# Retention scores times centred values: one fp32 product against three fp32r products of split parts, with the prompt's last 16 tokens stacked on 48 rows

## The chip, the cores and the metric

One NeuronCore of a Trainium2 chip runs one launch of the kernel. The metric is the device time of that launch in microseconds. The engines are TensorE (PE, with its weight loads shown apart as PEld), VectorE (DVE), ScalarE (ACT), GpSimd (POOL) and SyncE (SP, which issues most DMAs). Each works through its own queue in order, and the engines wait for each other through semaphores.

## The reference, cut to what matters

One step of a two-layer decoder: a pooling mixer, an MLP, a retention mixer with 8 heads, another MLP. 272 prompt tokens (16 of them learned) and 8 sample tokens run together. The change lies in the retention of the prompt:

```python
def retention_chunk(q, k, v, s, log_gamma):
    ...
    scores = jnp.einsum('bihd,bjhd->bhij', q, k) * decay[None]
    inner = jnp.einsum('bhij,bjhv->bihv', scores, v)
    ...
    s_new = s * s_dec[None, :, None, None] + jnp.einsum(
        'bjhd,bjhv->bhdv', k * k_dec[None, :, :, None], v).astype(s.dtype)
    return inner + cross, s_new

def retention_layer(x, pos, s, norm_g, w_in, w_out, log_gamma, n_lead):
    ...
    y = head_norm(o).reshape(b, t, RET_VDIM) * jax.nn.silu(g)   # head_norm: (o - mean) / std per head
    return x + y @ w_out, s
```

Since `head_norm` takes a mean over the 512 values of a head away from each token's output, the kernel takes that mean from each row of v first: "centred values". Scores times centred values is then the centred output of the prompt. The kernel computes the prompt in one piece (causal, 272 tokens) and not in chunks.

## The kernel before, in words

**Units.** The weights come as 388 units of 128x2048 numbers (1 MB, `raw`), loaded by SP in a fixed order (`ORDER`). Each unit is split in two halves: ACT casts a half to fp32r (`wh`, L130), DVE takes the rest (`wl`, L131), and TensorE multiplies in three products, `wh` by the activations' high part, `wl` by the high part, `wh` by the low part (`mm_acc`, L152): 48 products of 264 or 280 columns a unit. `begin_unit` splits two units ahead; `wh` and `wl` have four buffers each, so the half of a unit can be split once the same half of the unit two before has been used.

**Retention.** A head is four v units, two k, two q (the second of each makes the rotary embedding, `rope_unit`: two DVE products into `rpb`, then two POOL operations), four gate units g, and with heads 2, 4 and 7 (`PAIRED`) eight output units "oo", which multiply the outputs (`YH`, `YL`) of two earlier heads. Head 2 takes heads 0 and 1, head 4 takes 2 and 3, head 7 takes 5 and 6; head 7's own output is used in four "o" units after it. `v_tokens` turns v token by token (transposes, L466) in three groups `j` of 128, 128 and 16 tokens, and makes `vh`, `vl` (split v) and `vc` (centred, fp32). The last 16 tokens are copied six times side by side first (`tail_copies`), so that they stand on 96 rows. `attention(h)` is a generator that runs a step after each of the next twelve or so units: keys turned and split (L516), scores (L525) times decay (`pr`, L528), eight sample tokens (`sample`, L533 to L547: `kv` on ACT, state update and reductions on DVE), `prompt_o` (L555: per head two halves of two 128-value blocks `i`, each with three products for `j`), `prompt_state` (L565, L566), then the output's norm: the mean over samples (`om`, L587), the squares `osq` (ACT) summed by POOL (L597) between the gate products (L599), `token_rstd` (L196 to L206), `spread` (L210), and `oc`, `yh`, `yl` (L617 to L619).

**Order.** The program is written in the order of units, but a list scheduler of the tile framework moves instructions by its own estimate of when each is ready. So the order on each engine is fixed when the program is built, and a buffer that two tiles share orders their users. `tmp` with tag `sq` has two buffers, used in `prep` and for `osq`; `so`, `kv`, `rows` and `rpb` have buffers of their own (`kv` two).

Of the kernel before, what the change touches and what calls it, by code (L numbers as in the profile page):

```python
# [10 lines left out]
F32 = mybir.dt.float32  # L11
F32R = mybir.dt.float32r
# [4 lines left out]
P = 128  # L17
# [18 lines left out]
RT = (128, 128, 96)  # L36
# [47 lines left out]
def trunk_step(ctx: ExitStack, tc: tile.TileContext, wst, xT_d, xtok_d, spool_d, xc_d, xs_d, gains_d, gB_d, band_d, cs_d,  # L84
# [270 lines left out]
    with tc.tile_pool(name="rp", bufs=1) as rp, tc.tile_pool(name="rs", bufs=3) as rsp, \  # L355
# [45 lines left out]
        def rope_unit(h, kind, i, cols):  # L401
            parts = begin_unit(kind)
            w = cols.stop - cols.start
            ps = mm_tile(w)
            mm_acc(ps, parts, 0, XH, XL, cols)
            if i == 1:
                b = rp.tile([P, 2, C], F32, tag="rpb", name="rpb")
            else:
                cur[kind] = rp.tile([P, 2, C], F32, tag=kind + "T", name=f"{kind}T{h}")
            t = cur[kind] if i == 0 else b  # L410
            nc.vector.tensor_tensor(out=t[:, 0, :w], in0=ps, in1=(sin if i else cos)[:, cols], op=ALU.mult)
            nc.vector.tensor_tensor(out=t[:, 1, :w], in0=ps, in1=(cos if i else sin)[:, cols], op=ALU.mult)
# [37 lines left out]
        def v_tokens(h, j):  # L450
            vT = cur["v"]
            if j == 0:
# [4 lines left out]
                               for t, n, dt in (("vh", 3, F32R), ("vl", 2, F32R), ("vc", 3, F32))]  # L457
                cur["acc"] = rp.tile([P, 6], F32, tag="acc", name="acc")
                cur["vcols"] = token_cols(vT, 4)
            vh, vl, vc = cur["vtok"]  # L460
            acc = cur["acc"]
            nt, nr = JT[j][1], RT[j]
            rt = rtok[:nr, j:j + 1]
            ps = att_ps()
            for i in range(4):
                nc.tensor.transpose(ps[:nr, i * P:(i + 1) * P], cur["vcols"](i, j), ident)  # L466
# [5 lines left out]
        def split(hi, lo, ps, nr, scale, r0):  # L472

            rows = slice(0, nr)
            nc.scalar.activation(out=hi[rows], in_=ps[rows], func=AF.Copy, scale=scale)
            if nr < P:
                rows, lo = slice(r0, r0 + 32), hi
            nc.vector.scalar_tensor_tensor(out=lo[rows], in0=ps[rows], scalar=scale[rows],
                                           in1=hi[rows].bitcast(F32), op0=ALU.mult, op1=ALU.subtract)

        def attention(h, last):
            qT, kT, vs, (vh, vl, vc) = cur["q"], cur["k"], cur["vs"], cur["vtok"]
# [9 lines left out]
            rows = rp.tile([4 * NS, P], F32, tag="rows", name="rows")  # L492
# [18 lines left out]
            for j in range(3):  # L511
# [5 lines left out]
                split(kdh[:, j], kdl[:, min(j, 1)], ps[:, off:off + DK], RT[j], kvec[:RT[j], h, j:j + 1], 32)  # L517
# [3 lines left out]
            pr = rp.tile([P, DC], F32, tag="pr", name="pr")  # L521
            off = 0
            for j, (t0, nt, q0, nq) in enumerate(JT):
                for i in range(2):
                    nc.tensor.matmul(ps[:nt, off:off + nq], kT[:, i, t0:t0 + nt], qT[:, i, q0:q0 + nq], start=(i == 0),  # L525
                                     stop=(i == 1))
                off += nq
            nc.vector.tensor_tensor(out=pr[:, 0:400], in0=ps[:, 0:400], in1=dec[:, 0:400], op=ALU.mult)  # L528
            nc.vector.tensor_tensor(out=pr[:16, 400:416], in0=ps[:16, 400:416], in1=dec[:16, 400:416], op=ALU.mult)
# [19 lines left out]
            def prompt_o(half):  # L549
                ps = att_ps()  # L550
                for q in range(2):
                    i = half * 2 + q
                    off = 0
                    for j, (_, nt, q0, nq) in enumerate(JT):
                        nc.tensor.matmul(ps[:, q * 256 + q0:q * 256 + q0 + nq], vc[:nt, j, i * P:(i + 1) * P],  # L555
                                         pr[:nt, off:off + nq], start=(j == 0), stop=(j == 2))
                        off += nq
                nc.scalar.copy(out=OC[:, half * 2:half * 2 + 2, 0:256], in_=ps.rearrange("p (a b) -> p a b", a=2))

            def prompt_state(i):  # L560
# [5 lines left out]
                nc.tensor.matmul(ps, kdh[:96, 2, ds_], vh[:96, 2], start=False, stop=True)  # L566
                so = rp.tile([P, DV], F32, tag="so", name="so")
# [109 lines left out]
def constants():  # L677
# [22 lines left out]
    for h in range(H):  # L700
        off = 0
        for j, (t0, nt, q0, nq) in enumerate(JT):
            i = np.arange(q0, q0 + nq) + NMETA
            d = i[None, :] - (t0 + np.arange(nt))[:, None]
            dec[h, :nt, off:off + nq] = np.where(d >= 0, np.exp(np.maximum(d, 0) * LG[h]), 0.0) / 16.0
            kd = np.exp((NTOK - 1 - t0 - np.arange(nt)) * LG[h]) / 16.0
            kvec[:RT[j], h, j] = kd if j < 2 else np.tile(kd / 2.0, 6)
# [73 lines left out]
```

## Time and profile before

| | us |
|---|---|
| three timed runs, median (lowest to highest) | 2490.84 (2489.76 to 2491.4) |
| the profiled execution: its own time | 2488.74 |
| the span of its trace (first to last instruction) | 2487.0 |
| PE busy in the span | 2469.3 |
| DVE, ACT, POOL busy | 1513.0, 1152.6, 365.8 |
| the chain that ended last: "PE mm L152", the largest of the few that it follows | 30% of the span |

A start of a row in the timeline is the start of the first instruction of the group; the difference between two starts is the pace, while the duration of a matmul holds the pipeline's depth too. A plain fp32 matmul stands in the trace as two records, an fp32r matmul as one.

### The profile page before, as it was taken

To read this page: it belongs to the slowest core of one execution; us is meant where nothing else is said; L and a number is where in the kernel's file an instruction comes from. 1 tells how busy PE (TensorE), PEld (TensorE's weight loads), DVE (VectorE), ACT (ScalarE), POOL (GpSimd) and SP (SyncE) were. 2 spreads that over 40 slices of the span, in tenths; PEclk is the share of its full clock that TensorE was granted. 3 is DMA by queue.
4 is the path that set the end of the run, shared out by engine and by line. 5 is a ranking of instruction groups with operands and counts; after the bars stand their busy time and mean duration, and the time that the engine had idled before them with its cause. 6 is when DMAs were issued, how large, how long until landed. Compare 5 with 4: busy or idle time off the path is not lost. (4 is left out here: it accounts for less than half of the span.)

```text
span 2487.0 us, 46663 instructions
## 1 busy us (share of the span) xinstructions
PE 2469.3 (99%) x19560; PEld 2448.0 (98%) x19560; DVE 1513.0 (61%) x2400; ACT 1152.6 (46%) x1668; POOL 365.8 (15%) x280
## 2 busy tenths in 40 slices
PE   9999999999999999999999999999999999999998
PEld 9999999999999999999999999999999999999998
DVE  7554554554455567786778586788654654554553
ACT  5433333333334456664665565656433333333443
POOL 4210110120022101011010101102200200200222
PEclk9999999999999999999999999999999999999999
DMA  6444544444444557866668495885554455545453
GB/s 240 171 174 170 184 168 172 170 170 170 170 171 171 181 212 270 324 251 247 237 251 331 170 326 191 304 308 185 177 187 179 179 186 185 178 181 186 180 180 118
DMA packets 90182, 509.97 MB, mean 205 GB/s; under 512 B 10288, under 2 KB 11568, under 8 KB 39848
## 3 DMA queue, kind: packets, MB, share of 16 engines
q1 hardware_dynamic: 89507, 505.92, 56.3%
q8 instruction: 153, 2.51, 0.4%
q10 hardware_dynamic: 432, 0.95, 0.1%
q14 instruction: 58, 0.48, 0.1%
q0 software_dynamic: 32, 0.12, 0.0%
HBM read 466.72 MB, written 41.15 MB: 204 GB/s over the span
## 5 line engine op out<-in xcount | busy, mean ns | idle before, releaser
L130 ACT CAST wh<-raw 128x1024 fp32r<-128x1024 f32 x776 | 799.8, 1050 | 1181.9 <-PE mm L152 660.0
L131 DVE TENSOR_TENSOR wl<-raw,wh 128x1024 fp32r<-128x1024 f32 x776 | 1000.5, 1321 | 101.8 <-ACT wh L130 100.8
L152 PE MATMUL mm<-xh,wh 128*128 128x280 f32 (+1 forms) x3584 | 491.6, 289 | 0.0
L152 PE MATMUL mm<-xl,wh 128*128 128x280 f32 (+1 forms) x3584 | 488.8, 288 | 0.1
L152 PE MATMUL mm<-xh,wl 128*128 128x280 f32 (+1 forms) x3584 | 487.1, 287 | 0.0
L152 PEld LDWEIGHTS mm<-xh,wh 128*128 128x128 f32 x3584 | 463.2, 188 | 1.8 <-ACT wh L130 0.2
L152 PEld LDWEIGHTS mm<-xl,wh 128*128 128x128 f32 x3584 | 463.3, 188 | 0.6 <-DVE xl L174 0.3
L152 PEld LDWEIGHTS mm<-xh,wl 128*128 128x128 f32 x3584 | 462.7, 188 | 0.3
L322 POOL TENSOR_TENSOR hf<-r 128x280 f32<-128x280 f32 (+1 forms) x128 | 185.3, 1448 | 1154.6 <-DVE r L318 1154.6
L348 DVE TENSOR_TENSOR xT<-mm,xT 128x280 f32<-128x280 f32 (+1 forms) x128 | 56.4, 441 | 401.4 <-PE mm L152 401.4
L152 PE MATMUL mm<-hh,wh 128*128 128x280 f32 (+1 forms) x2048 | 276.3, 287 | 0.0
L152 PE MATMUL mm<-hh,wl 128*128 128x280 f32 (+1 forms) x2048 | 276.2, 287 | 0.0
L152 PE MATMUL mm<-hl,wh 128*128 128x280 f32 (+1 forms) x2048 | 276.2, 287 | 0.0
L152 PEld LDWEIGHTS mm<-hh,wh 128*128 128x128 f32 x2048 | 263.8, 188 | 0.0
L152 PEld LDWEIGHTS mm<-hh,wl 128*128 128x128 f32 x2048 | 263.8, 188 | 0.0
L152 PEld LDWEIGHTS mm<-hl,wh 128*128 128x128 f32 x2048 | 263.7, 188 | 0.0
L318 DVE SCALAR_TENSOR_TENSOR r<-mm,rstd 128x280 f32<-128x280 f32 (+1 forms) x128 | 56.2, 440 | 303.5 <-PE mm L152 303.4
L540 ACT ACTIVATE kv<-bc,vs 128x256 f32<-128x256 f32 x256 | 110.0, 499 | 39.8 <-DMA bc<-rd 36.6
L545 DVE CUSTOM_DVE_ANT_0 bc<-s,bc 128x256 f32<-128x256 f32 x256 | 103.2, 417 | 2.0
L542 DVE SCALAR_TENSOR_TENSOR s<-s,kv 128x512 f32<-128x512 f32 x128 | 86.2, 684 | 21.6 <-ACT kv L540 20.2
L170 POOL TENSOR_TENSOR ssq<-ssq,sq 128x280 f32<-128x280 f32 (+1 forms) x56 | 71.1, 1269 | 180.9 <-ACT sq L168 160.7
L599 POOL TENSOR_TENSOR oc<-oc,gs 128x264 f32<-128x264 f32 x32 | 31.8, 1007 | 322.2 <-ACT ssq L593 322.2
(179 smaller groups left out, 1504.2 us busy)
## 6 DMA issues: line engine op xcount, KB each, us to landing
raw<-in_wst SPq DMA_DIRECT2D x388, 1024.0 KB, 4.9
s<-in_sret SPq DMA_DIRECT2D x64, 512.0 KB, 5.3
out_rs<-s SPq DMA_DIRECT2D x64, 512.0 KB, 7.0
bc<-rd SPq DMA_DIRECT2D x64, 256.0 KB, 8.8
out_rp<-so SPq DMA_DIRECT2D x16, 256.0 KB, 5.4
xT<-in_xT SPq DMA_DIRECT2D x4, 560.0 KB, 15.1
dec<-in_dec SPq DMA_DIRECT2D x8, 208.0 KB, 6.5
xa<-in_xtok SPq DMA_DIRECT2D x1, 1024.0 KB, 7.0
```

Of the source, the lines that this page charges most:

```text
L130: nc.scalar.copy(out=wh, in_=src)
L131: nc.vector.tensor_tensor(out=wl, in0=src, in1=wh.bitcast(F32), op=ALU.subtract)
L152: nc.tensor.matmul(ps, parts[s][z][:, kk, :], rhs[k][:, cols], start=(j == 0), stop=(j == len(todo) - 1))
L170: nc.gpsimd.tensor_tensor(out=ssq[:, cols], in0=ssq[:, cols], in1=sq[:, :w], op=ALU.add)
L318: nc.vector.scalar_tensor_tensor(out=r[:, :T], in0=ps, scalar=0.0, in1=rstd[:, cols], op0=ALU.max, op1=ALU.mult)
L322: nc.gpsimd.tensor_tensor(out=hf[:, :T], in0=r[:, :T], in1=r[:, :T], op=ALU.mult)
L348: nc.vector.tensor_tensor(out=xT[:, n, cols], in0=ps, in1=xT[:, n, cols], op=ALU.add)
L540: nc.scalar.activation(out=kv[:, i, :], in_=bc[:, 256:512], func=AF.Copy, scale=vs[:, 2 * z + i, b:b + 1])
L542: nc.vector.scalar_tensor_tensor(out=s[:, 2 * z:2 * z + 2], in0=s[:, 2 * z:2 * z + 2], scalar=GAMMA[h], in1=kv, op0=ALU.mult, op1=ALU.add)
L545: nc.vector.tensor_tensor_reduce(out=bc[:, 256:512], in0=s[:, i, :], in1=bc[:, 0:256], op0=ALU.mult, op1=ALU.add, scale=1.0, scalar=0.0, a ...
L599: nc.gpsimd.tensor_tensor(out=OC[:, i], in0=OC[:, i], in1=gates[h][:, i], op=ALU.mult)
```

## The change

- `vc` (fp32) is replaced by `vch`, `vcl` (its fp32r split), and `pr` by `prh`, `prl`; `pr` itself is now written over the decay table `dec`. `prompt_o` does three fp32r products for `j` = 0 and 1 and one for `j` = 2.
- For `j` = 2 the 16 tokens stand three times on 48 rows (before: six times on 96), and high and low parts are laid out on the three copies so that one product holds all three terms. This goes for the keys and values in `prompt_state` too; the transposes of the tail have 48 columns where they had 96, and the last score product has 48 columns where it had 16.
- `split` is rewritten, with one more DVE instruction for the keys' tail.
- Buffers are shared where they had been separate: `rows`, `so` and the scratch of `v_tokens` for `j` = 0 and 2 use one `so` buffer, the scratch for `j` = 1 takes a `kv` buffer, and the rotary `rpb` takes the two `sq` buffers of `tmp`.

```diff
-RT = (128, 128, 96)
+RT = (128, 128, 48)
...
             if i == 1:
-                b = rp.tile([P, 2, C], F32, tag="rpb", name="rpb")
+                b = [tmp.tile([P, C], F32, tag="sq", name="rpb")[:, :w] for _ in range(2)]
...
-            nc.scalar.activation(out=vc[:nt, j], in_=ps[:nt], func=AF.Copy, scale=rt[:nt], accum_out=acc[:nt, j:j + 1])
-            split(vh[:, j], vl[:, min(j, 1)], ps, nr, rt, 64)
-            nc.vector.tensor_scalar_mul(acc[:nt, 3 + j:4 + j], acc[:nt, j:j + 1], -1.0 / DV)
-            nc.scalar.activation(out=vc[:nt, j], in_=vc[:nt, j], func=AF.Identity, bias=acc[:nt, 3 + j:4 + j])
+            t = scratch(j)[:nr]
+            nc.scalar.activation(out=t, in_=ps, func=AF.Copy, scale=rt, accum_out=acc)
+            split(vh[:nr, j], vl[:nr, min(j, 1)], ps, rt, ALU.mult, False)
+            nc.vector.tensor_scalar_mul(neg, acc, -1.0 / DV)
+            split(vch[:nr, j], vcl[:nr, min(j, 1)], t, neg, ALU.add, False)
+
+        def scratch(j=0):
+            return rp.tile([P, DV], F32, tag="kv" if j == 1 else "so", name="so", bufs=2 if j == 1 else 1)
+
+        def split(hi, lo, x, s, op, left):
+            kw = {"func": AF.Copy, "scale": s} if op is ALU.mult else {"func": AF.Identity, "bias": s}
+            nc.scalar.activation(out=hi, in_=x, **kw)
+            rows = slice(0, P)
+            if hi.shape[0] < P:
+                rows, lo = slice(0, 32) if left else slice(32, 48), hi
+            nc.vector.scalar_tensor_tensor(out=lo[rows], in0=x[rows], scalar=s[rows], in1=hi[rows].bitcast(F32),
+                                           op0=op, op1=ALU.subtract)
+            if hi.shape[0] < P and left:
+                nc.vector.tensor_scalar_mul(hi[:16], x[:16], s[:16])
...
+            nc.vector.tensor_tensor(out=pr[:, hd], in0=ps[:, hd], in1=dec[:, hd], op=ALU.mult)
+            nc.scalar.copy(out=prh[:, hd], in_=pr[:, hd])
+            nc.vector.tensor_tensor(out=pr[:tr, tl], in0=ps[:tr, tl], in1=dec[:tr, tl], op=ALU.mult)
+            nc.vector.tensor_copy(prh[:tr, tl], pr[:tr, tl])
+            nc.vector.tensor_tensor(out=prh[:32, tl], in0=pr[:32, tl], in1=prh[:32, tl].bitcast(F32), op=ALU.subtract)
+            nc.vector.tensor_copy(prh[:16, tl], pr[:16, tl])
+            nc.vector.tensor_tensor(out=prl[:, hd], in0=pr[:, hd], in1=prh[:, hd].bitcast(F32), op=ALU.subtract)
...
-                    for j, (_, nt, q0, nq) in enumerate(JT):
-                        nc.tensor.matmul(ps[:, q * 256 + q0:q * 256 + q0 + nq], vc[:nt, j, i * P:(i + 1) * P],
-                                         pr[:nt, off:off + nq], start=(j == 0), stop=(j == 2))
+                    for j, (_, _, q0, nq) in enumerate(JT):
+                        for m, (a, b) in enumerate(((vch, prh), (vch, prl), (vcl, prh))[:3 if j < 2 else 1]):
+                            nc.tensor.matmul(ps[:, q * 256 + q0:q * 256 + q0 + nq], a[:RT[j], j, i * P:(i + 1) * P],
+                                             b[:RT[j], off:off + nq], start=(j + m == 0), stop=(j == 2))
...
-                nc.tensor.matmul(ps, kdh[:96, 2, ds_], vh[:96, 2], start=False, stop=True)
-                so = rp.tile([P, DV], F32, tag="so", name="so")
+                nc.tensor.matmul(ps, kdh[:RT[2], 2, ds_], vh[:RT[2], 2], start=False, stop=True)
+                so = scratch()
```

The shared buffers move instructions. Line numbers of the changed kernel are some 1 to 15 higher (L210 stays, L411 now stands for both rotary products, L491 becomes L497, L525 L533, L555 L570, L566 L581, L587 L602, L588 L603, L597 L612, L617 L632).

On PE in head 2, from the last products of its first gate unit (`xl`) to the first product with head 1's output (before `yh_11520`, after `yh_11593`; `yh_10480` and `yh_10521` are head 0's); before:

```order
L210 MATMUL sp<-dg,ones 128x264
...
L152 MATMUL mm<-xl_108,wh_1_11458 128x264
L152 MATMUL mm<-yh_10480,wh_0_11534 128x264 x2
L491 MATMUL att<-ident,qk 32x128
L516 MATMUL att<-ident,kT_11241 128x128 x2
L516 MATMUL att<-ident,tail 96x128 x2
L152 MATMUL mm<-yh_10480,wh_0_11534 128x264 x2
L152 MATMUL mm<-yh_10480,wh_1_11538 128x264 x4
L152 MATMUL mm<-yh_10480,wh_0_11637 128x264 x4
L152 MATMUL mm<-yh_11520,wh_0_11534 128x264
```

The same place after:

```order
L152 MATMUL mm<-yh_10521,wh_1_11611 128x264 x4
L196 MATMUL st<-mean_v,ssq 88x1 x3
L152 MATMUL mm<-yh_10521,wh_0_11711 128x264 x4
L152 MATMUL mm<-yh_10521,wh_1_11715 128x264 x4
L497 MATMUL att<-ident,qk 32x128
L522 MATMUL att<-ident,kT_11305 128x128 x2
L522 MATMUL att<-ident,tail 48x128 x2
L533 MATMUL att<-qT_11509,kT_11305 128x256 x2
...
L522 MATMUL att<-ident,kT_11305 128x128 x2
L210 MATMUL sp<-dg,ones 128x264
L570 MATMUL att<-prh,vch_11312 128x256 x2
L152 MATMUL mm<-yh_11593,wh_0_11607 128x264
```

The `spread` of head 1's norm (L210) stood before the oo units with some 17 products of other work behind it; now it stands behind the whole front of head 2's attention and directly ahead of the product that needs its result. The norm's first step (L196) moved from the second q unit into the first oo unit. Head 4 has the same two orders.

On DVE, the same place, from the subtraction of head 1's sample mean to the copy of head 2's q columns (`qk`), before:

```order
L588 TENSOR_TENSOR oc_10668<-os,om 128x4x8
...
L131 TENSOR_TENSOR wl_0_11455<-raw_11190,wh_0_11454 128x1024
L131 TENSOR_TENSOR wl_1_11459<-raw_11190,wh_1_11458 128x1024
L200 TENSOR_SCALAR rs<-st 88x3
...
L411 TENSOR_TENSOR rpb<-mm,cs 128x264
L412 TENSOR_TENSOR rpb<-mm,cs 128x264
L131 TENSOR_TENSOR wl_0_11535<-raw_11293,wh_0_11534 128x1024
L204 TENSOR_TENSOR dg<-ident,rs 88x264
L131 TENSOR_TENSOR wl_1_11539<-raw_11293,wh_1_11538 128x1024
L488 COPY qk<-qT_11437 128x16
```

After (`wl_0_11527`, `wl_1_11531` are the gate unit's halves, as `wl_0_11455`, `wl_1_11459` before):

```order
L131 TENSOR_TENSOR wl_0_11527<-raw_11254,wh_0_11526 128x1024
L601 TENSOR_REDUCE om<-os 128x8
L131 TENSOR_TENSOR wl_1_11531<-raw_11254,wh_1_11530 128x1024
L603 TENSOR_TENSOR oc_10716<-os,om 128x4x8
L131 TENSOR_TENSOR wl_0_11608<-raw_11362,wh_0_11607 128x1024
L131 TENSOR_TENSOR wl_1_11612<-raw_11362,wh_1_11611 128x1024
L411 TENSOR_TENSOR rpb<-mm,cs 128x264 x2
L423 TENSOR_TENSOR gs_11666<-mm,rstd 128x264
L131 TENSOR_TENSOR wl_0_11712<-raw_11458,wh_0_11711 128x1024
L131 TENSOR_TENSOR wl_1_11716<-raw_11458,wh_1_11715 128x1024
L200 TENSOR_SCALAR rs<-st 88x3
L494 COPY qk<-qT_11509 128x16
```

L588 stood ahead of two halves of the gate unit and now, as L603, behind them; `rpb` stood behind the norm's small operations (L200 on) and now ahead of them, and two more halves stand between it and `qk`.

On PE at the end of head 7, from the norm of its output to its first use (before `yh_18919`), before:

```order
L196 MATMUL st<-mean_v,ssq 88x1 x3
L152 MATMUL mm<-yh_17976,wl_1_18773 128x264 x2
...
L152 MATMUL mm<-yh_16646,wl_1_18860 128x264 x2
L210 MATMUL sp<-dg,ones 128x264
L152 MATMUL mm<-yh_16646,wl_1_18860 128x264 x2
L152 MATMUL mm<-yh_17976,wl_1_18860 128x264 x4
L152 MATMUL mm<-yl_16647,wh_1_18859 128x264 x4
L152 MATMUL mm<-yl_17977,wh_1_18859 128x264 x4
L152 MATMUL mm<-yh_18919,wh_0_18934 128x264 x2
```

After:

```order
L152 MATMUL mm<-yl_16839,wh_1_19115 128x264 x4
L152 MATMUL mm<-yl_18210,wh_1_19115 128x264 x4
L196 MATMUL st<-mean_v,ssq 88x1 x3
L210 MATMUL sp<-dg,ones 128x264
L152 MATMUL mm<-yh_19175,wh_0_19190 128x264 x2
```

Between L196 and L210 stood 44 products of unit work, and 14 between L210 and the first use; now there is none.

## Rows read from the trace of the kernel before

**Rows 1.** The page, busy time of each engine, share of the span, instructions.
```profile
PE 2469.3 (99%) x19560; PEld 2448.0 (98%) x19560; DVE 1513.0 (61%) x2400; ACT 1152.6 (46%) x1668; POOL 365.8 (15%) x280
```
**Rows 2.** Timeline of PE (start, us, line, shape, count): half of head 0's prompt output.
```profile
923.73 1.86 PE L152 MATMUL mm<-xl,wh 128*128 128x264 f32 x14
925.42 2.36 PE L555 MATMUL att<-pr,vc 128*128 128x256 f32 x12
927.71 2.21 PE L152 MATMUL mm<-xh,wh 128*128 128x264 f32 x16
929.76 0.52 PE L152 MATMUL mm<-xh,wl 128*128 128x264 f32 x3
```
**Rows 3.** Timeline of PE: the last product of a state block of head 0.
```profile
943.59 0.39 PE L566 MATMUL att<-vh,kd 96*128 96x512 f32 x1
943.82 2.22 PE L152 MATMUL mm<-xh,wh 128*128 128x280 f32 x16
```
**Rows 4.** Timeline of PEld: the weight loads there.
```profile
943.36 0.19 PEld L566 LDWEIGHTS att<-vh,kd 96*128 96x128 f32 x1
943.60 1.57 PEld L152 LDWEIGHTS mm<-xh,wh 128*128 128x128 f32 x11
```
**Rows 5.** Timeline of PE in the pooling stage: products on 128, 110 and 54 rows.
```profile
41.94 0.37 PE L280 MATMUL dps<-band,xb 128*128 128x113 f32 x2
42.15 0.33 PE L282 MATMUL dps<-band,xc 110*128 110x39 f32 x2
42.31 0.47 PE L279 MATMUL dps<-band,xa 128*128 128x128 f32 x2
42.61 0.37 PE L280 MATMUL dps<-band,xb 128*128 128x113 f32 x2
42.92 0.41 PE L284 MATMUL dps<-band,xc 54*128 54x31 f32 x2
43.25 0.39 PE L285 MATMUL dps<-band,xs 128*128 128x8 f32 x2
```
**Rows 6.** Timeline of PEld there: the loads for 54 rows.
```profile
42.91 0.29 PEld L284 LDWEIGHTS dps<-band,xc 54*128 54x128 f32 x2
```
**Rows 7.** Timeline of PEld and PE: a product with 32 columns of weights, head 0.
```profile
910.97 0.14 PEld L491 LDWEIGHTS att<-ident,qk 128*32 128x32 f32 x2
910.97 0.30 PE L491 MATMUL att<-ident,qk 128*32 128x128 f32 x1
```
**Rows 8.** Timeline of PE: head 2's first gate unit starts.
```profile
1076.43 2.09 PE L152 MATMUL mm<-xh,wh 128*128 128x264 f32 x16
```
**Rows 9.** Timeline of DVE there.
```profile
1065.68 0.17 DVE L588 TENSOR_TENSOR oc<-os,om 128x32 f32<-128x32 f32 x1
...
1076.62 0.43 DVE L411 TENSOR_TENSOR rpb<-mm,cs 128x264 f32<-128x264 f32 x1 [0.18 <-PE mm L152]
```
**Rows 10.** Timeline of POOL there: first and last of seven operations on head 1's output.
```profile
1067.19 0.91 POOL L599 TENSOR_TENSOR oc<-oc,gs 128x264 f32<-128x264 f32 x1 [0.79 <-ACT ssq L593]
...
1072.62 1.72 POOL L597 TENSOR_TENSOR ssq<-ssq,osq 128x264 f32<-128x264 f32 x1
```
**Rows 11.** The page, costliest groups: ACT's and DVE's part of the weight split (busy, mean ns).
```profile
L130 ACT CAST wh<-raw 128x1024 fp32r<-128x1024 f32 x776 | 799.8, 1050 | 1181.9 <-PE mm L152 660.0
L131 DVE TENSOR_TENSOR wl<-raw,wh 128x1024 fp32r<-128x1024 f32 x776 | 1000.5, 1321 | 101.8 <-ACT wh L130 100.8
```
**Rows 12.** Timeline of PE: head 7's norm starts; the first use of its output waits.
```profile
1695.52 0.56 PE L196 MATMUL st<-mean_v,ssq 128*88 128x1 f32 x6
...
1705.16 0.88 PE L152 MATMUL mm<-yh,wh 128*128 128x264 f32 x5 [0.26 <-ACT yh L618]
```
**Rows 13.** Timeline of ACT: ahead of the square root in head 7's norm.
```profile
1695.09 1.28 ACT L182 ACT_TABLE_LOAD   x1
```
**Rows 14.** Timeline of PE: the longest wait in the trace, in the pooling stage.
```profile
19.99 0.77 PE L280 MATMUL dps<-band,xb 128*128 128x113 f32 x2 [3.99 <-DVE band L257]
```
**Rows 15.** Busy time by stretch: us, PE, PEld, DVE, ACT, POOL (counts), granted clock, DMA share, GB/s.
```profile
20.00:26.00 6.00, 6.00 (x28) 6.00 (x29) 3.67 (x6) 4.41 (x12) 5.90 (x2) 0.50 1.02 424
```

More of the change, by code (lines that the diff above doesn't have):

```diff
@@ L363, in trunk_step @@
         rtok = rp.tile([P, 3], F32, name="rtok")
-        cos, sin = cs[:, 0], cs[:, 1]
         def tail_copies(src, n):
-            t = rp.tile([P, 4, 6, 16], F32, tag="tail", name="tail")[:, :n]
-            nc.scalar.copy(out=t, in_=src[:, :, JT[2][0]:NTOK].unsqueeze(2).to_broadcast([P, n, 6, 16]))
+            t = rp.tile([P, 4, 3, 16], F32, tag="tail", name="tail")[:, :n]
+            nc.scalar.copy(out=t, in_=src[:, :, JT[2][0]:NTOK].unsqueeze(2).to_broadcast([P, n, 3, 16]))
             return t.rearrange("p n r t -> p n (r t)")
@@ L469, in v_tokens @@
-            nc.vector.tensor_scalar_mul(acc[:nt, 3 + j:4 + j], acc[:nt, j:j + 1], -1.0 / DV)
-            nc.scalar.activation(out=vc[:nt, j], in_=vc[:nt, j], func=AF.Identity, bias=acc[:nt, 3 + j:4 + j])
[L472 to L479, printed above, removed]
+                nc.tensor.transpose(ps[:, i * P:(i + 1) * P], cur["vcols"](i, j), ident)
@@ L516, in attention @@
                     nc.tensor.transpose(ps[:RT[j], off + i * P:off + (i + 1) * P], cols(i, j), ident)
-                split(kdh[:, j], kdl[:, min(j, 1)], ps[:, off:off + DK], RT[j], kvec[:RT[j], h, j:j + 1], 32)
+                nr = RT[j]
+                split(kdh[:nr, j], kdl[:nr, min(j, 1)], ps[:nr, off:off + DK], kvec[:nr, h, j:j + 1], ALU.mult, True)
             yield True
             ps = att_ps()
-            pr = rp.tile([P, DC], F32, tag="pr", name="pr")
+            prh, prl = [rp.tile([P, DC], F32R, tag=t, name=t) for t in ("prh", "prl")]
+            pr = dec
             off = 0
@@ L524, in attention @@
                 for i in range(2):
-                    nc.tensor.matmul(ps[:nt, off:off + nq], kT[:, i, t0:t0 + nt], qT[:, i, q0:q0 + nq], start=(i == 0),
+                    nc.tensor.matmul(ps[:RT[j], off:off + nq], cols(i, j), qT[:, i, q0:q0 + nq], start=(i == 0),
                                      stop=(i == 1))
                 off += nq
-            nc.vector.tensor_tensor(out=pr[:, 0:400], in0=ps[:, 0:400], in1=dec[:, 0:400], op=ALU.mult)
-            nc.vector.tensor_tensor(out=pr[:16, 400:416], in0=ps[:16, 400:416], in1=dec[:16, 400:416], op=ALU.mult)
+            hd, tl, tr = slice(0, 400), slice(400, DC), RT[2]
+            nc.vector.tensor_tensor(out=pr[:, hd], in0=ps[:, hd], in1=dec[:, hd], op=ALU.mult)
[5 more added lines that the diff above has]
+            nc.vector.tensor_tensor(out=prl[:, hd], in0=pr[:, hd], in1=prh[:, hd].bitcast(F32), op=ALU.subtract)
             OC = rp.tile([P, 4, CQ], F32, tag="oc", name=f"oc{h}")
@@ L704, in constants @@
             d = i[None, :] - (t0 + np.arange(nt))[:, None]
-            dec[h, :nt, off:off + nq] = np.where(d >= 0, np.exp(np.maximum(d, 0) * LG[h]), 0.0) / 16.0
-            kd = np.exp((NTOK - 1 - t0 - np.arange(nt)) * LG[h]) / 16.0
-            kvec[:RT[j], h, j] = kd if j < 2 else np.tile(kd / 2.0, 6)
+            n = RT[j] // nt
+            de = np.where(d >= 0, np.exp(np.maximum(d, 0) * LG[h]), 0.0) / 16.0
+            dec[h, :RT[j], off:off + nq] = np.tile(de, (n, 1))
+            kvec[:RT[j], h, j] = np.tile(np.exp((NTOK - 1 - t0 - np.arange(nt)) * LG[h]) / 16.0, n)
             off += nq
```

26 lines of the change are left out of this document (12 added, 14 removed).

## The prediction

> **What bounds the kernel now.** I read the busy times first, then TensorE's timeline around the retention work, then the engines that feed it. TensorE is busy for 2469.3 of 2487.0 us [rows 1], so the end is set by how long its instructions take plus whatever it waits, and it hardly waits: at the first use of head 7's output, one of the most exposed places, it lost 0.26 us [rows 12]. DVE is busy for 61% and ACT for 46% [rows 1]. So a microsecond of matmul saved is a microsecond off the end, and one more instruction on DVE or ACT costs nothing, unless TensorE has to stand still for it.
>
> The pace on TensorE: 264 columns of fp32r take (929.76 - 927.71) / 16 = 0.128 us behind the attention block [rows 2] and (925.42 - 923.73) / 14 = 0.121 us elsewhere; 512 columns take 0.23 us [rows 3]. That is close to linear, so 256 columns cost about 0.118 us. Short products are bounded by the weight load: six products of 113 to 39 columns with six loads take 42.61 - 41.94 = 0.67 us [rows 5], 0.11 us each, which I use for a load of 128 columns.
>
> A load normally runs ahead: the one of the 96-row product stands at 943.36 us, its product at 943.59, and the next load at 943.60 for a product at 943.82 [rows 3, 4]. It doesn't where the array's shape changes. The 54-row product's load starts at 42.91 us with the product itself at 42.92 [rows 5, 6], and so does the load with 32 columns of weights (both at 910.97) [rows 7]. The pair of 54 rows and the pair before it take 43.25 - 42.61 = 0.64 us, the like pairs with 110 rows 42.31 - 41.94 = 0.37 us [rows 5]: entering and leaving a 54-row product costs at least 0.27 us. Between wide products, whose length hides the load of the next, both loads come into the open as well: two drains of some 0.09 us (0.31 against 0.21 us for the pair that is left behind) and two loads of 0.11 make 0.40 us. I take 0.40 and keep 0.27 for the range. The Trainium skill, TensorEngine Tiling (Array Packing), section Tiling Modes, says that changing the tiling mode drains TensorE, and lists 64 rows and 64 columns as modes; rows 5 to 7 agree.
>
> **The change part by part: TensorE's work.**
> 1. Prompt output. A half takes 927.71 - 925.42 = 2.29 us, and its last switch (16 rows) makes the following 16 products 0.11 us longer [rows 2]: 2.40 us, 16 times, 38.4 us. After, per block `i`: three products of 256 columns, 0.35; two of 144 bounded by the load, 0.22; the last of them and its drain, 0.15; the load for 48 rows, its 16 columns and the drain, 0.21; the next load, 0.11. That is 1.04 us, 2.08 a half: 0.32 saved, 5.1 us in all. If 48 rows make no switch it would be 3 x 0.118 + 4 x 0.11 = 0.79 a block, and 13.0 us saved.
> 2. Prompt state. The 96-row product becomes a 48-row one, 16 times. Before, it makes no switch [rows 3, 4]; after, two: 16 x 0.40 = 6.4 us (4.3 at 0.27).
> 3. The transposes of the tail: 48 columns for 96, in 16 groups (one for v, one for k in each head). No row shows 48 columns; 32 make a switch [rows 7], and on the side of the rows 54 do and 96 don't [rows 4, 6]. I side with 32: with the shorter load on entering, 0.34 each, 5.4 us (0 if 48 columns behave like 96, 4.3 at 0.27).
> 4. The third score product has 48 columns for 16; its switch is there already, four longer loads a head: 0.6 us.
>
> Together -5.1 + 6.4 + 5.4 + 0.6 = **+7.3 us** of TensorE. The added products of parts and the one fewer fp32 product are all in 1.
>
> **The other engines' work.** Per head DVE gets `vcl` (three operations of 0.7 us), `prl` and four small ones, some 3.5 us of a head's 96; ACT gets `prh` and smaller tails; POOL and SP keep their counts. At 61% and 46% this hides [rows 1], except for its place in the queue.
>
> **The order around the shared buffers.** Sample 7's second `kv` needs a buffer that the next head's `v_tokens` now holds, so with heads 0, 1, 3 and 6 (four tail units, too few for all the steps) the sample mean comes later. In the order, L602 stands 0.9 into head 2's second q unit, 0.6 us before its first gate unit, which starts at 1076.43 in the old trace [rows 8]. So L603 can't come before about 1076.2, where L588 came at 1065.68 [rows 9]. POOL's seven operations on the output took from 1067.19 to 1074.34, 7.15 us [rows 10]. The second `rpb` buffer is that of the last `osq`, which POOL releases at their end: 1076.43 + 7.3. Before, `rpb` waited for nothing but its product [rows 9]. DVE's queue stands still for it, and with it the oo unit's halves, the norm's start and `qk`: an operation of 264 columns takes 0.43 us and a small one 0.17 [rows 9], a half of the split 1.32 [rows 11], so `rpb`, the gate, two halves and two small ones make `qk` ready 7.3 + 0.9 + 2.6 + 0.3 = 11.1 us after the gate unit's start. TensorE gets there after 48 + 16 products of 0.121 and L196, 7.75 + 0.56 [rows 12] = 8.3 us. **It waits 2.8 us**, 3 with the turn of `qk` itself. Then it does the scores, the turned keys and L210, and needs a free accumulator for L570: that is held by the keys, whose DVE split stands behind the four L632, which wait for L210: some five operations of 0.36 to 0.43, **1.8 us** more. 4.8 us in head 2, the same in head 4. In heads 1 and 7 no unit needs the output so soon, and `qk` comes in time; I take 0.
>
> At the end of head 7, L196 and L210 stand next to each other, with nothing in between. ACT finishes a half of the split, 1.05 [rows 11], loads a table, 1.28 [rows 13], and takes the root (0.2, put at a small operation); DVE makes five small steps and the diagonal, 5 x 0.17 + 0.43 = 1.3 [rows 9]: 3.8 us, of which L196 itself fills 0.5, so 3.3 of waiting; then `oc` and `yh`, 0.8 [rows 9]. Less the 0.26 of before [rows 12]: **3.8 us**.
>
> Together 2 x 4.8 + 3.8 = **+13.4 us**, bounds 2 (all of it hidden but for a part at the end) and 26 (double).
>
> **The sum.** The profiled execution took 2488.74 us, of which the span is 2487.0; 2.1 below the median of three. 2488.74 + 7.3 + 13.4 = 2509.4 by the profiled execution, and 2511.5 against the median of 2490.84, which is my forecast: 0.8% slower.
>
> **The rivals.**
> - *No switch for 48 rows and columns*, faster. A 48-row product runs as the 96-row one does. Then 1. saves 13.0 and 2. to 3. cost nothing: -13.0 + 0.6 = -12.4 us, and if the waits too stay under some 2 us, 2480. For it: 96 rows show no switch [rows 4]. Against: 54 rows do [rows 5, 6], and 48 is farther from 96. It decides alone as long as the waits stay below 7.4 us. With the waits of 13.4 the same mechanism gives 2492, no change. The Trainium skill, TensorE: Matmul & The Clock Gate, section Why this matters for your kernels, says a matmul with a small K takes the time of K=128, which is this rival; rows 5 speak against it where neighbours are wide.
> - *The switches, but no waits*: DVE has the results ready in time as before, when the margin was small [rows 12]. +7.3 to 9: 2499. For it: every place like this was hidden before. Against: the pair L196, L210 leaves nothing to hide behind.
> - *The clock falls in a wait.* After the 3.99 us wait in the pooling stage [rows 14] the granted clock stood at 0.50 for 20 to 26 us [rows 15], the lower of its two levels (1.2 GHz), which cost half of some 6 us. If it falls in all three waits, +9 to 10: 2521. Against: the new waits are shorter (3 us, then work).
> - *The parts are no cheaper than fp32*: three fp32r products take what two fp32 records did. The change then saves nothing in 1., +5: 2516; the pace of L152 [rows 2] speaks against it.
>
> **How the numbers follow.** The forecast, switches and waits of 4 to 25 us: 0.60. Switches without waits: 0.15. No switch and no waits: 0.06. No switch, with waits: 0.09. The clock falls, or more goes late: 0.08. Parts no cheaper: 0.02. The two cases without a switch are left out below, so the range goes from 2498 (the switches at 0.27 us and hardly a wait: 2490.84 + 4 + 3) to 2526 (the waits doubled, or the clock fallen). A measurement of this kernel can tell about 0.2%, 5 us, from no change. Slower by more than that: 0.60 + 0.12 + 0.08 + 0.02 + 0.02 = 0.84; within: 0.03 of the second and 0.06 of the fourth, 0.09; faster: 0.06 and 0.01 of the fourth, 0.07.
>
> **What would show it.** In the new trace the L581 load starts with its product instead of 0.2 us ahead, and the next unit's load too; the tail's transposes likewise. A half of the prompt output takes about 2.1 us. TensorE waits some 3 us at L497 in heads 2 and 4 and again before L570, and 3 to 4 us between L196 and L210 behind the last oo unit, while DVE's row before `rpb` names POOL. I am wrong if the loads of 48 rows run ahead, if L497 finds `qk` ready, or if TensorE stands still in other heads.

## The result and the profile after

The changed kernel takes 2507.02 us (median of 6 runs, 2504.09 to 2509.52), the kernel before 2490.70 (2489.76 to 2491.83): 1.0064 times as long, 95% interval 1.0051 to 1.0077, or 16.3 us slower. The forecast was 2511.5, 20.7 us slower. The profiled execution is the slowest of the six: 2509.52 us, its span 2507.7.

The page's busy line answers to [rows 1]:

```profile
PE 2479.7 (99%) x19592; PEld 2451.5 (98%) x19592; DVE 1536.4 (61%) x2464; ACT 1154.9 (46%) x1676; POOL 361.8 (14%) x280
```

TensorE is busy for 10.4 us longer in a span that is 20.7 us longer, so only about half can be work; the rest is standing still. Its list of waits (engine, line, what it waited for: us in total, times, longest) names the places:

```profile
PE dps L280 <- DVE band L257: 5.2, 1, 5.2
PE att L497 <- DVE qk L494: 4.0, 2, 2.0
PE sp L210 <- DVE dg L204: 3.8, 1, 3.8
PE mm L152 <- ACT yh L633: 1.3, 2, 1.0
PE att L570 <- ACT prh L538: 0.7, 2, 0.5
```

The first stands at the start, which the change doesn't touch (3.99 us in [rows 14]; the kernels below, with the same start, show 3.9 to 5.5). The other four are new or larger, and heads 1 and 7 are not among them.

**TensorE's own work.** The timeline of PE (start, us, engine, line, shape, count) in one half of the prompt output of head 0, answering to [rows 2]:

```profile
935.83 0.28 PE L570 MATMUL att<-prh,vch 128*128 128x256 f32 x1
...
936.56 0.59 PE L570 MATMUL att<-prh,vch 48*128 48x16 f32 x2
...
937.81 1.43 PE L152 MATMUL mm<-xh,wh 128*128 128x280 f32 x9
```

From its first product to the next unit it takes 1.98 us, where [rows 2] has 2.29; with 0.11 for the load behind the last switch, as there, 2.09. The prompt state's last product, PE and then PEld, answering to [rows 3, 4]:

```profile
945.60 0.50 PE L581 MATMUL att<-vh,kd 48*128 48x512 f32 x1
946.03 0.79 PE L152 MATMUL mm<-xh,wh 128*128 128x280 f32 x4
```

```profile
945.59 0.18 PEld L581 LDWEIGHTS att<-vh,kd 48*128 48x128 f32 x1 [0.36 <-issue]
946.02 0.69 PEld L152 LDWEIGHTS mm<-xh,wh 128*128 128x128 f32 x5 [0.25 <-issue]
```

Both loads now start with their products (945.59 and 945.60, 946.02 and 946.03), where with 96 rows each came 0.2 us ahead. This is the switch that was forecast.

**The wait in head 2.** Rows of DVE and PE from the timeline, in order of time; the brackets hold the idle time before a row and what ended it:

```profile
1077.25 0.19 DVE L603 TENSOR_TENSOR oc<-os,om 128x32 f32<-128x32 f32 x1 [0.90 <-PE om L602]
...
1077.77 2.11 PE L152 MATMUL mm<-xh,wh 128*128 128x264 f32 x16
...
1083.56 0.43 DVE L411 TENSOR_TENSOR rpb<-mm,cs 128x264 f32<-128x264 f32 x1 [2.07 <-POOL ssq L612]
...
1084.99 0.43 DVE L411 TENSOR_TENSOR rpb<-mm,cs 128x264 f32<-128x264 f32 x1 [0.99 <-POOL ssq L612]
1085.01 0.63 PE L196 MATMUL st<-mean_v,ssq 128*88 128x1 f32 x6 [0.30 <-POOL ssq L612]
...
1085.68 2.91 DVE L131 TENSOR_TENSOR wl<-raw,wh 128x1024 fp32r<-128x1024 f32 x2
...
1088.58 0.16 DVE L494 COPY qk<-qT 128x16 f32<-128x16 f32 x1
...
1088.80 0.64 PE L497 MATMUL att<-ident,qk 128*32 128x128 f32 x2 [2.02 <-DVE qk L494]
```

The subtraction of the sample mean stands 0.5 us ahead of the gate unit's start (1077.25 and 1077.77), where it stood 10.8 us ahead of it before (1065.68 and 1076.43, [rows 8, 9]). DVE stands still for POOL before both halves of `rpb`, then has two halves of the split in its queue, and the turned queries come 2.0 us too late.

**The wait at the end of head 7**, all engines, answering to [rows 12, 13]:

```profile
1716.52 0.56 PE L196 MATMUL st<-mean_v,ssq 128*88 128x1 f32 x6
...
1717.78 1.28 ACT L182 ACT_TABLE_LOAD   x1
...
1720.87 1.22 PE L210 MATMUL sp<-dg,ones 88*128 88x264 f32 x2 [3.79 <-DVE dg L204]
...
1723.12 3.23 PE L152 MATMUL mm<-yh,wh 128*128 128x264 f32 x13 [1.04 <-ACT yh L633]
...
1726.15 0.72 PE L152 MATMUL mm<-yh,wl 128*128 128x264 f32 x4
```

The last two rows are the price of something else: 13 products in 3.03 us (1723.12 to 1726.15) are 0.23 each, nearly twice the pace of [rows 2]. The table by stretches (from:to, its length, busy us of PE, PEld, DVE, ACT and POOL, granted clock, share of the DMA engines, GB/s) shows why:

```profile
1084.00:1088.00 4.00, 2.47 (x20) 2.06 (x19) 3.01 (x4) 2.54 (x3) 2.37 (x4) 1.00 0.41 172
1088.00:1094.50 6.50, 5.70 (x22) 4.38 (x22) 3.64 (x14) 1.62 (x5) 0.00 (x0) 0.50 0.67 246
1313.00:1316.50 3.50, 3.22 (x11) 2.38 (x12) 2.24 (x11) 1.35 (x4) 0.00 (x0) 0.54 0.70 232
1719.00:1726.00 7.00, 4.09 (x15) 3.38 (x16) 4.08 (x15) 1.69 (x6) 0.00 (x0) 0.53 0.43 153
```

Behind each of the three waits the granted clock stands at 0.50 to 0.54, the lower of its two levels (1.2 GHz), as in [rows 15]. The rival that gave the clock a chance of 0.08 came true in this execution beside the forecast, not in its place.

### The profile page after: what moved, and what is told of

Its sections match the earlier page's. It is cut to its first block, busy times and chain, and to the rows that moved or that the text cites. A ratio compares the mean times of both kernels' runs of the same rounds, so it can differ in the third digit from the quotient of the medians.

```text
span 2507.7 us, 46816 instructions
## 1 busy us (share of the span) xinstructions
PE 2479.7 (99%) x19592; PEld 2451.5 (98%) x19592; DVE 1536.4 (61%) x2464; ACT 1154.9 (46%) x1676; POOL 361.8 (14%) x280
## 4 chain that ended last, share of the span: by engine, by line
PE 96%; DVE 2%; DMA 1%; POOL 1%; ACT 0%; issue 0%; SPq 0%; DVEq 0%; ACTq 0%
PE mm L152 91%; PE att L570 1%; PE att L580 1%; PE att L533 1%; DMA u<-in_gB 1%; DVE wl L131 1%; DVE xl L174 0%; PE att L464 0%; POOL oc L614 0%; PE att L522 0%; PE att L581 0%; PE sp L210 0%; PE st L196 0%; DVE xT L432 0%; PE dps L280 0%
## 5 line engine op out<-in xcount | busy, mean ns | idle before, releaser
L152 PE MATMUL mm<-xh,wh 128*128 128x280 f32 (+1 forms) x3584 | 493.1, 289 | 0.2 <-ACT xh L163 0.2
L152 PE MATMUL mm<-xh,wl 128*128 128x280 f32 (+1 forms) x3584 | 489.5, 288 | 0.0
L152 PE MATMUL mm<-xl,wh 128*128 128x280 f32 (+1 forms) x3584 | 488.1, 287 | 0.4 <-DVE xl L174 0.4
L152 PEld LDWEIGHTS mm<-xh,wh 128*128 128x128 f32 x3584 | 463.2, 188 | 3.4 <-issue 1.2
L152 PEld LDWEIGHTS mm<-xl,wh 128*128 128x128 f32 x3584 | 463.0, 188 | 0.7 <-DVE xl L174 0.6
L152 PEld LDWEIGHTS mm<-xh,wl 128*128 128x128 f32 x3584 | 463.4, 188 | 0.3
L152 PE MATMUL mm<-hh,wh 128*128 128x280 f32 (+1 forms) x2048 | 276.3, 287 | 0.0
L152 PE MATMUL mm<-hh,wl 128*128 128x280 f32 (+1 forms) x2048 | 276.2, 287 | 0.0
L152 PE MATMUL mm<-hl,wh 128*128 128x280 f32 (+1 forms) x2048 | 276.2, 287 | 0.0
L152 PEld LDWEIGHTS mm<-hh,wh 128*128 128x128 f32 x2048 | 263.8, 188 | 0.0
L152 PEld LDWEIGHTS mm<-hh,wl 128*128 128x128 f32 x2048 | 263.8, 188 | 0.0
L152 PEld LDWEIGHTS mm<-hl,wh 128*128 128x128 f32 x2048 | 263.7, 188 | 0.0
L556 DVE SCALAR_TENSOR_TENSOR s<-s,kv 128x512 f32<-128x512 f32 x128 | 86.2, 683 | 17.5 <-ACT kv L554 16.3
```

The source lines that it names most:

```text
L152: nc.tensor.matmul(ps, parts[s][z][:, kk, :], rhs[k][:, cols], start=(j == 0), stop=(j == len(todo) - 1))
L556: nc.vector.scalar_tensor_tensor(out=s[:, 2 * z:2 * z + 2], in0=s[:, 2 * z:2 * z + 2], scalar=GAMMA[h], in1=kv, op0=ALU.mult, op1=ALU.add)
```

## Experiments

Each kernel is the changed kernel with the edits shown; times are medians.

**1. The tail on 96 rows again.**

```
-RT = (128, 128, 48)
+RT = (128, 128, 96)
-    t = rp.tile([P, 4, 3, 16], F32, tag="tail", ...)
+    t = rp.tile([P, 4, 6, 16], F32, tag="tail", ...)
+    on = (np.arange(RT[j]) < 3 * nt)      # tables: copies 4 to 6 are zero
```

> The changed kernel with the prompt's last 16 tokens on 96 rows instead of 48: six copies, of which the tables make the last three zero, so that the result is the same sum. TensorE's order around the waits is unchanged. My theory (a product of 48 rows between wide ones makes TensorE switch its shape, one of 96 rows doesn't): the state's block goes from 2.03 back to 1.63 us (16 times, -6.4), a half of the prompt output from 2.09 to about 1.6 us (16 times, -8), the waits in heads 2 and 4 and at the end of head 7 stay: 2507 - 14 = 2493 us. Rival (the price comes with the added products or with the stacking itself, whatever the number of rows): both blocks stay at 2.03 and 2.09 us, 2507 us. Half of each: only one of the two blocks gets shorter, 2499 to 2501.

Measured: 2493.70 us, 13.3 less than the changed kernel. The waits are unchanged (4.0 us at L497, 3.8 at L210). PEld at the state's last product:

```profile
943.34 0.19 PEld L581 LDWEIGHTS att<-vh,kd 96*128 96x128 f32 x1
943.57 0.82 PEld L152 LDWEIGHTS mm<-xh,wh 128*128 128x128 f32 x5
```

That product starts at 943.57 and the next unit at 943.81, so both loads run ahead again. The switch belongs to the number of rows.

**2. One of the two narrow products back.** With 96 rows everywhere, the prompt output reads only 48 of them.

```
-    a[:RT[j], j, ...], b[:RT[j], off:off + nq]
+    a[:(128, 128, 48)[j], j, ...], b[:(128, 128, 48)[j], off:off + nq]
```

> The changed kernel with the tail on 96 rows (the last three of six copies zero), of which the prompt state's product reads all 96 and the prompt output's only the first 48, so that one of the two narrow products is back alone. TensorE's order is that of the changed kernel. Switch theory: the state's block at 1.63 us as with 96 rows, a half of the output at 2.09 as with 48; against the 96 rows everywhere (2493.7) +16 x 0.45 to 0.5 = +7 to 8: 2501. Rival (what the 96 rows gained was one thing, such as earlier results or a steadier clock, and not two products each at its price): within 2 us of 2493.7 or of 2507.

Measured: 2500.51 us. The state alone is worth 2507.02 - 2500.51 = 6.5 us, the output's narrow product 2500.51 - 2493.70 = 6.8, each with an uncertainty of some us, since the changed kernel's own executions lie 5.4 us apart. The blocks in the traces are firmer: from the first product to the next unit the state's takes 1.64 us as in the kernel of 1. (1.93 in the changed kernel), a half of the output 1.99 as in the changed kernel (1.98; 1.52 in the kernel of 1.). Two products, each at its price.

**3. Where the switch begins: 64 and 32 rows.** As in 1., with 64, and with 32.

> The tail on 64 rows and 64 columns (four copies, the last one zero); the same order on TensorE. It is to say where the switch begins. If the array has a shape of its own up to 64 rows: the state's block 2.03 us, the load of the 64 rows starts with its product; a half of the output 2.09. If the price belongs to 48 as an odd number of rows: 1.63 and 1.6. The third score product with 64 columns: 1.84 us for the scores of a head as with 48, where 96 columns gave 1.75, if columns behave as rows do; the transposes with 64 columns 0.44 us for four, as with 48 and 96. One execution, with the waits of the changed kernel: about 2507 by the first, 2493 by the second.

> The tail on 32 rows and 32 columns: two copies, so that one of the three partial products of the last 16 tokens is left out (the value's low part), and with it one small DVE operation per piece. The mean stands elsewhere in the order, so only the blocks are compared, not the time. If 32 rows are in the same shape as 48: the state's block 2.03 us, a half of the output 2.09, the loads with their products. If narrower is a further shape with its own price: 2.1 or more. The transposes with 32 columns: 0.44 us for four if a transposition never changes the shape; 0.6 or more if it does below 48, as the turned queries with 32 columns at L497 seem to show.

Measured in one execution each: 2509.42 us with 64 rows. At 32 rows the mean stands elsewhere, so its 2503.64 isn't compared. From the last unit product before to the first behind, the state's block takes 2.05 us with 32, 48 and 64 rows (12, 16 and 16 such blocks) and 1.77 with 96; with 0.11 in the load behind it the price is 0.4. PEld with 64 rows, whose product starts at 945.51 and the next unit at 945.94:

```profile
945.51 0.18 PEld L581 LDWEIGHTS att<-vh,kd 64*128 64x128 f32 x1 [0.36 <-issue]
945.94 0.69 PEld L152 LDWEIGHTS mm<-xh,wh 128*128 128x128 f32 x5 [0.25 <-issue]
```

So it isn't 48 as an odd number, and narrower isn't dearer. On the side of the columns the same kernels split. The tail's transposes with 32 columns, first PEld, then PE:

```profile
893.46 0.44 PEld L464 LDWEIGHTS att<-ident,tail 128*32 128x32 f32 x4
```

```profile
893.58 0.60 PE L464 MATMUL att<-ident,tail 128*32 128x128 f32 x4
```

The load runs 0.12 us ahead: no switch, at 32, 48, 64 or 96 columns (four of them 0.48 to 0.49 us in each of these four kernels). The third score product is no transposition. In the changed kernel, with 48 columns:

```profile
921.58 0.25 PEld L533 LDWEIGHTS att<-qT,tail 128*48 128x48 f32 x4
```

```profile
921.58 0.35 PE L533 MATMUL att<-qT,tail 128*48 128x16 f32 x4
```

Its load starts with it; with 96 columns, in the kernel of 1., the load stands at 920.63 and the product at 920.75. The scores of a head take 1.85 us with 48 columns, 1.91 with 64, 1.76 with 96.

**4. The mean on time.**

```
-    t = scratch(j)[:nr]      # j = 1: one of sample 7's two "kv" buffers
+    t = scratch()[:nr]       # always the buffer of the other pieces
```

> The changed kernel with one buffer moved: the second piece of the head's values goes through the buffer of the other two pieces instead of one of sample 7's two; 48 rows and the rpb buffers shared with the squares stay. My theory (the late sample mean is what makes TensorE wait): the mean stands before the second q unit again, TensorE's wait at L497 in heads 2 and 4, the one before L570 and the 3.8 us between L196 and L210 at the end of head 7 go, and with them the three stretches at a granted clock of 0.5 that follow: -6 -5 -6 us, 2490 us. Rival 1 (the waits alone count, the stretches at the lower clock are hidden behind other engines): about -9, 2498. Rival 2 (the buffers that rpb shares with the squares, or DVE's added work, make the waits whenever the mean comes): the wait at L497 stays at 2 us, only the end of head 7 is gained, 2501.

Measured: 2494.44 us, 12.6 less than the changed kernel; 1.0017 times the kernel before (1.0009 to 1.0026). The mean is back ahead of the second q unit, 0.45 us later than the 1065.68 of [rows 9]:

```profile
1066.13 0.18 DVE L603 TENSOR_TENSOR oc<-os,om 128x32 f32<-128x32 f32 x1
```

In the eight heads one line of waits is left above 0.3 us:

```profile
PE st L196 <- POOL ssq L612: 1.8, 4, 0.5
```

and the three places run at full clock:

```profile
1055.00:1110.00 55.00, 54.69 (x439) 53.53 (x438) 49.15 (x107) 35.73 (x61) 12.86 (x11) 1.00 0.70 239
1285.00:1335.00 50.00, 49.49 (x397) 48.19 (x396) 46.04 (x98) 32.56 (x56) 12.64 (x11) 1.00 0.70 251
1690.00:1740.00 50.00, 49.60 (x394) 48.04 (x393) 42.59 (x72) 31.95 (x59) 17.69 (x18) 1.00 0.42 153
```

The `rpb` buffers are still shared with the squares here, and nothing waits for them: the late mean is the cause, the shared squares only carry it.

**5. Products in the waits.**

```
+    fill_gap(4 if h in (1, 3) else 0, sq)      # behind L196, 128x264, ones by the squares
+    fill_gap(7 if last else 0, sq)             # before L210
```

> The changed kernel with products put into the three long waits, whose results nothing reads: four in heads 2 and 4 behind L196, seven at the end of head 7 between L196 and L210. They shorten no wait. Theory (the granted clock falls because TensorE stands still, and the work after the wait pays for it): the clock stays at 1.00 through the three places, where it was 0.50 for 6.8, 3.4 and 6.8 us, and half of that comes back: 2507 - 8.5 = 2498.5. Rival 1 (in those stretches TensorE waits for DVE and ACT anyway): the clock stays up, but the gain is under 3 us, 2504 or more. Rival 2 (the clock falls for another reason, the load on the memory for instance): the stretches at 0.50 stay, 2507 or a little more.

Measured: 2504.93 us (2503.56 to 2509.59), 1.0059 of the kernel before (1.0046 to 1.0071): by the times not to be told from the changed kernel. The trace is clearer. The stretch of head 2 stays at full clock:

```profile
1055.00:1110.00 55.00, 53.67 (x419) 51.37 (x418) 44.51 (x99) 35.76 (x65) 10.67 (x11) 1.00 0.63 224
```

and so do the other two. What the three places cost can be read by comparing when the same L152 product starts, at a calm point before and behind the place (there are equally many of them in each kernel), against the kernel of 4., which has no waits there:

| profiled execution | head 2 | head 4 | end of head 7 | together |
|---|---|---|---|---|
| changed kernel | 5.7 | 4.6 | 7.1 | 17.4 us |
| waits filled, clock up | 3.7 | 3.8 | 5.1 | 12.6 us |

In these places of the profiled executions the clock is 4.8 us of the price, and the waits with what goes with them are 12.6. Between the places both kernels are 2.0 us faster than the kernel of 4., so that from 60 us to the last unit product the late mean costs 15.3 us in the changed kernel and 10.6 with the clock held up. By medians it is 12.6 (2507.02 - 2494.44) and 10.5 (2504.93 - 2494.44).

At the lower level stood 6.8 + 3.4 + 6.8 = 17 us. TensorE was busy in some 13 of them (5.70, 3.22 and 4.09, above), and half of that is 6.5; why 1.7 of it don't show in the 4.8 is open.

That the clock gives back less by medians, 2.1 us, has a reason in the executions that weren't profiled: each comes with its mean granted clock, and that isn't the same in all. Of the changed kernel's six, two have 0.993 (2509.52, the profiled one, and 2508.38 us) and four 0.995 (2504.09 to 2507.12). The kernel of 1., with the same order around the same waits, has eleven: 0.996 at 2488.53 and 2489.59 us, 0.992 at 2494.84 to 2496.04, the others between. So one kernel's clock falls for longer in some executions than in others, and there the difference is some 6 us.

**6. `rpb` in other buffers**, the mean still late.

```
-    b = [tmp.tile([P, C], F32, tag="sq", name="rpb")[:, :w] for _ in range(2)]
+    b = [scratch()[:, :w], tmp.tile([P, C], F32, tag="dg", name="rpb", bufs=1)[:, :w]]
```

> The changed kernel with the two rpb halves in two other buffers (the one of the values' pieces and the one of the norm's diagonal) instead of the squares'; sample 7's buffers stay shared, so the mean stays late. My theory (DVE stood still because rpb waits for POOL's last sum): DVE's row before rpb no longer names POOL and waits under 0.3 us, TensorE's wait at L497 in heads 2 and 4 goes. But the order now puts L196 and L210 only four products apart there, so that the chain of the root and the diagonal is open: about 3 us of waiting at L210 in each of the two heads in its place, and 3.8 at the end of head 7 as before: 2504 to 2508 us. Rival (DVE's queue itself, not POOL, makes the turned queries late): 2 us at L497 stay, 2507 to 2510.

Measured: 2515.44 us, 8.4 more than the changed kernel and 7.4 above the range that was expected. The wait at L497 did go, and neither half of `rpb` names POOL's sum any more. But what came in its place is larger. From the list of waits:

```profile
PE sp L210 <- DVE dg L204: 6.8, 3, 2.8
...
PE st L196 <- POOL ssq L612: 3.9, 1, 3.9
PE st L196 <- DVE ssq L612: 2.0, 1, 2.0
```

L210 waits in all three places, as expected, though only 1.15 us in head 2 (2.84 and 2.83 in the others). But L196 now comes before its squares are there, in head 2 and at the end of head 7, which I had not reckoned with, and the second half of `rpb` stands behind L210, which reads the buffer that it was moved to (1.41 us in heads 2 and 4). With the mean late, the norm's chain was open in this order too, in other places; a third place for `rpb` wasn't tried.

**7. Both causes removed**: the edits of 1. and 4. together.

> Both edits: 96 rows, and the second piece of the values kept out of sample 7's buffers. If the two causes are independent, the gains add: 2507 - 14 - 17 = 2476 us, and against the kernel before this is the prompt output's saving alone (2.40 to 1.6 us, 16 times, -13): 2478. Rival (TensorE gets through its work so much sooner that it meets DVE's queue again): a wait at L497 or before the state's products comes back, 2483 or more.

Measured: 2478.01 us, 0.9949 of the kernel before (0.9936 to 0.9963), 12.6 us faster than it. No wait at L497, no stretch at the lower clock between the start and the end. By medians 13.3 + 12.6 = 25.9 of the 29.0 between this and the changed kernel are the two gains. In the profiled executions, from 60 us to the last unit product, they are 14.8 and 15.3 us, and both together 31.0: all but 0.9 adds up, so most of the 3.1 that is missing by medians is the spread between executions, in which the clock has its part (5.).

**8. One more narrow product widened**, on the kernel of 7.: the turned queries' weights get 40 columns of zeros.

```
-    qk = rp.tile([P, 2, 2, NS], ...)
+    qw = rp.tile([P, 72], ...); nc.gpsimd.memset(qw[:, 32:], 0.0)
-    nc.tensor.matmul(ps[:4 * NS, 0:P], qk..., ident, ...)
+    nc.tensor.matmul(ps[:72, 0:P], qw, ident, ...)
```

> The version with 96 rows and the mean on time, and one more narrow product widened: the turned queries' block, 32 columns of weights, gets 40 columns of zeros, 72 in all, so that the product that turns them is wide; its added rows are not read. TensorE's order is unchanged. Transposes didn't switch at 48 or 32 columns, while the third score product did at 48 and not at 96, and this product is of the second kind (a product, no transposition). Theory (any product with few columns of weights switches): the load of the 72 columns runs ahead by some 0.1 us, the block of this product and the four transposes behind it goes from 0.96 to 0.7 us, 8 times: -2 us against the version without it, 2476. Rival (the load starts with its product because it waits for the turned queries, not because of a switch): no change in the block, 2478.

> The version with 96 rows and the mean on time once more, for the comparison with the widened queries on the same chip: 2478 us; no wait at L497, no stretch at a granted clock of 0.5 between the start and the end.

Measured: 2476.86 us, the kernel of 7. beside it 2477.37. PEld with 72 columns, whose product starts at 911.20, and then with 32, whose product starts at 912.37 as its load does:

```profile
911.08 0.27 PEld L499 LDWEIGHTS att<-ident,qk 128*72 128x72 f32 x2
```

```profile
912.37 0.14 PEld L497 LDWEIGHTS att<-ident,qk 128*32 128x32 f32 x2
```

The load of 72 columns runs 0.12 us ahead. The block of this product and the four transposes goes from 0.963 to 0.697 us, in all eight heads, 2.1 us; the medians differ by 0.5, which the runs' spread of 1 to 2 us doesn't settle. The start with the product, from which I had read a switch at 32 columns, is a switch and no wait for the queries.

## Why the prediction was right, and where not

**The sign and the size** held: the change is slower, by 16.3 us for 20.7. By medians it splits where the forecast split it: the kernel with the mean on time is 2494.44 - 2490.61 = 3.8 us slower than before (forecast for TensorE's work 7.3), and the late mean costs another 12.6 (forecast 13.4). That both parts came out so near is in part luck, as the terms show.

1. **Prompt output**: 2.08 us forecast for a half, 2.09 measured; 16 x 0.31 = 5.0 us saved. Right, and so is its other branch: without a switch 13.0 us were to be saved, and the kernel of 7. saves 12.6.
2. **Prompt state**: +6.4 forecast at 0.40 us for a lone narrow product, 6.5 measured by undoing it alone, and 16 x 0.40 by its blocks.
3. **The tail's transposes**: +5.4 forecast, nothing measured. This is the step that failed. The prediction sided with [rows 7], 32 columns, against 96, and took a product for a transposition: L491 turns the queries with an ordinary product by the identity. The Trainium skill, TensorEngine Tiling (Array Packing), section Gotcha 2: Feature Incompatibilities, lists the transpose mode with FP32 or FP32R input as mutually exclusive with column tiling; I had not weighed it. The traces agree: transposes of 32, 48 and 64 columns keep the wide shape, and the ordinary products of 32, 48 and 64 columns don't.
4. **The third score product**: +0.6 forecast, 8 x 0.09 = 0.7 measured.

Together +2.2 instead of +7.3; 1.6 us of the 3.8 are beyond it. 0.5 lie in longer waits of L196 for POOL (1.8 for the 1.3 before); the rest isn't located.

5. **Heads 2 and 4**: 4.8 us each forecast. The chain is right row by row (POOL, `rpb`, two halves of the split, `qk`): `qk` was ready 11.0 us after the gate unit's start, for 11.1. TensorE got there after 9.0 us and not after 8.3, 0.3 of it its own wait for POOL at L196, and so the wait at L497 was 2.0 for 2.8. The 1.8 before L570 was mis-sized: its row names ACT's `prh`, not the accumulator, and it and the wait for `yh` behind it are some 0.5 us. With the clock held up a head costs 3.7 to 3.8; what that has beyond these 2.5 us wasn't taken apart.
6. **End of head 7**: 3.8 us forecast. The chain behind L196 took the 3.8 us worked out, but none of it ran beside L196, for which 0.5 had been taken off, and `yh` took 1.0 for 0.8. With the clock held up 5.1 us.
7. **The clock**: a rival with +9 to 10, half of three stretches of some 6 us. In the profiled execution they were 6.8, 3.4 and 6.8 us and cost 4.8, in part because TensorE was busy in only some 13 of the 17. By medians the filled waits give back 2.1 us, within the spread; most of the six executions had less of it than the profiled one (5. above).

So misses met. Of TensorE's work 5.4 us were too much, for the transposes, and 1.6 came that no term held. For the late mean 13.4 us of waits stood in the sum where 10.5 were measured with the clock held up, and the clock, which the sum left out, brought 2.1 by medians. Where the rivals gave a time, building them gave it: no switch with the waits 2492 forecast and 2493.7 measured, no switch and no waits 2480 and 2478.0. "Switches, but no waits" was 2499 and is 2494.4, lower by the transposes. The products of parts by themselves gain 12.6 us; the 48 rows and one shared buffer lose more than that.

The Trainium skill, TensorE: Matmul & The Clock Gate, section Why this matters for your kernels, gives a single matmul with K=32 the time of K=128. Here the 48-row product takes 0.43 us to the next start (945.60 to 946.03) and the 96-row one 0.24 (943.57 to 943.81), so between wide products the measurement decides against it.

## What to carry to other kernels

Between wide products, pad a narrow one (64 rows or columns and fewer) with zeros; here 96 rows, and 72 or 96 columns, were enough. A lone product of 32 to 64 rows cost 0.40 us, one with 32 columns 0.27, and the padding cost nothing on TensorE; fp32 transposes need none. When a change shares buffers, follow each new owner to the next thing that waits for it, and then to the order in which the work is now issued: one buffer (2 KB on each partition) put off a mean by less than two units of work and cost 12.6 us. Where TensorE is the bound, price a wait with the clock behind it, but only for the work that stands there, and expect it to differ between executions.

## What the runs showed of the hardware beyond the forecast

- The switch has the same price at 32, 48 and 64 rows (the state's block 2.05 us each, 1.77 at 96). In the kernel before, loads of 70 and 88 rows at L210 run ahead of their products (79.73 and 79.86, 1081.26 and 1081.38), so by this sign the switch ends between 64 and 70 rows; what a 70-row product costs wasn't measured.
- Ordinary fp32 products switch with 32, 48 and 64 columns of weights, and don't with 72 and 96; fp32 transposes with 32, 48, 64 and 96 columns all load ahead of themselves.
- The granted clock fell behind a wait of only 2.0 us at L497, with 8 products and a wait of 0.30 us just ahead of it, and stood at 0.50 from 1088 to 1094.5 us; with four unread products in the same place it stayed at 1.00.
- A wait of that length doesn't always bring the clock down. The kernel with 32 rows waits 2.30 us at the same line, before its first output product, in head 2 and in head 4: the clock stays at 1.00 behind the first and stands at 0.50 for 3.4 us behind the second (from 1310.5). The kernel of 1., with the changed kernel's order around the waits, has 3.4 us at 0.50 in head 2 and 6.8 in head 4, the changed kernel 6.8 and 3.4.
